# A hybrid attention trunk on one core: gate projections one pair ahead, zeros multiplied first, another place for one load

## The chip, the cores and the metric

One core of a Trainium2 chip runs the whole kernel. The metric is the time of one execution on the device, in microseconds (us); lower is better. Engines are named as in the profile: PE is TensorE (PEld its weight loads), DVE VectorE, ACT ScalarE, POOL GpSimd, SP the engine whose queue issues the DMAs.

## The reference

1024 tokens of width 1024 pass through two residual layers and a final RMSNorm. The first layer, in which the change lies, is

```python
h = rmsnorm(x, norm_w[0])
qa, ka, va, qb, kb, vb, z = jnp.split(h @ w_in, splits, axis=-1)
oa, _ = banded_attention(qa, ka, va, bias_a, band_a, sinks)          # 8 heads, window 128
for window, dil in ((128, 1), (512, 4), (2048, 16)):                 # 8 heads, dilated
    o, lse = banded_attention(to_strided(qb, dil), to_strided(kb, dil), to_strided(vb, dil), ...)
ob = sum(softmax(lses) * outs)
x = x + (concat([oa, ob]) * silu(z)) @ w_out
```

Each branch output is multiplied by a gate, silu of the projection z, before the output projection. The second layer is multi-head latent attention with 16 heads and a gate of its own.

## The kernel before, in words

**Precision.** Every large product is made of three matmuls: each operand is split into a high part and a rest, and `mm3` (lines 116 to 118) adds high x high, rest x high and high x rest in one bank of PSUM. A split is a copy on ACT (line 96) and a subtraction on DVE (101, 103) or POOL (111).

**First phase, to about 94 us.** For each of 8 blocks of 128 tokens: load x (`load_x`, line 322), sum of squares on ACT (124), a power on POOL (126), scaling on DVE (129), eight transposes on PE (137), the split into hH and hL, and the value projection of the dilated heads (24 matmuls into `ot`), which goes to DRAM. The eight weight tiles of that projection (`load_v`, 311) are loaded during block 0; the load of block 1 is issued after the sixth of them. DVE also makes the tables of sines and cosines in this phase.

**Projections.** `tproj` makes one 128-column projection of all tokens: two weight loads (`wst`), splits of them, and 8 blocks x 3 products x 2 halves of the tokens = 48 matmuls of 512 columns into `tp`. `proj_qk(pr)` makes q and k of a pair of heads (96 matmuls for the first four pairs, 48 for the last four), `proj_z(pr)` its gate (48, then tanh on ACT, line 178, and a product on DVE, 179).

**Heads.** There are 8 pairs. The dilated heads are pairs 0 to 3, the sliding-window heads pairs 4 to 7. A dilated head has eight groups of scores (four natural, four strided); a group is four matmuls into one bank `sc` (lines 225 and 226), per region of the bank a reduction on DVE that adds the bias and finds the maximum (229), and an exponential on ACT (232) that frees the bank; there are two such banks. Then the two softmaxes are merged: a small matmul (601), vector work, and a second small matmul (628), called the merge matmul here, whose result DVE reads as x (630). The values follow: POOL scales the probabilities (237), PE transposes them (188, bank `pt`), ACT and DVE split the transposes (96, 101), and PE multiplies by v (204, bank `ot`).

**Order.** Work is written as lists of pieces. At step n the values of head n are interleaved with the scores of head n+1, and the list `fill` is the projection work that PE can do meanwhile: q and k of the next pair at even n, the gate of the own pair at odd n, the gate of pair 7 at n = 14. The table `WAIT` holds some pieces of `fill` back behind named matmuls. A scheduler then places the pieces on the engines' queues by its own model of their durations; what order came out is shown below. Each engine takes its queue in order. `finish(pr)` multiplies the gate into the pair's output and stores it.

**Buffers.** The pool `gp` has one buffer for a gate, `sp` two for the natural bias `b1` and two for its copy `b1r`. A table of 128 x 824 numbers is loaded as `pm`, of which 4 and 32 columns are used.

Of the kernel before, what the change touches and what calls it, by code (L numbers as in the profile page):

```python
# [20 lines left out]
SEQ = 1024  # L21
P = 128
# [269 lines left out]
def layer0(c, x, norm_w, rel_bias, w_in, w_out, onehot, band, perm, x1d, tables, before_out, x1_done):  # L292
# [12 lines left out]
    with tc.tile_pool(name="ph1", bufs=1, reuse_waits="tile", side="right") as p1:  # L305
# [20 lines left out]
        for t in range(NT):  # L326
            xs = p1.tile([P, D], F32, name="xs", tag="xs", bufs=2)
            rms_rows(c, p1, xts[t], w0, xs, xs, 1 if t else 2)
            to_hT(c, xs, t, hH, hL)
            if t == 0:  # L330
                for d in range(ND):
                    load_v(d)
                    if d == 5:
                        load_x(1)
            elif t + 1 < NT:
                load_x(t + 1)
            ps = c.bank("ot")
            m = None
            tt = slice(t * P, (t + 1) * P)
            for d in range(ND):  # L340
                m = c.mm3(ps, hH[:, d, tt], hL[:, d, tt], wv[d][0], wv[d][1], d == 0, d == ND - 1, m)
            vt = p1.tile([P, 8, P], F32R, name="vt", tag="vt", bufs=2)
            src = ps.rearrange("p (h e) -> p h e", h=8)
            c.copy(vt[:, :, :HD], src, 0.5)
            c.low(vt[:, :, HD:], src, vt[:, :, :HD], 0.5)
            dma.dma_start(vd[tt], f(vt))
# [32 lines left out]
    def tl(pool, shape, dt, tag, bufs):  # L379
        return pool.tile(shape, dt, name=tag, tag=tag, bufs=bufs)  # L380

    pm = sp.tile([P, 4 * P + 312], F32, name="pm")
    dma.dma_start(pm, perm)


    o = 4 * P
    quarter, unsel = pm[:, o + 8:o + 12], pm[:, o + 24 + 192 + 64:o + 24 + 192 + 96]
    same = sp.tile([P, R4, RA], F32, name="same")
    V.tensor_reduce(same[:, 0], c.ident.rearrange("p (b a) -> p a b", a=RA), axis=AX.X, op=ALU.add)
    V.tensor_copy(same[:, 1:], same[:, 0:1].to_broadcast([P, R4 - 1, RA]))  # L390
    same = same.rearrange("p r a -> p (r a)")

    def bias_tile(h, cfg, tag, quarters=False):
        b = tl(sp, [P, 256], F32, tag, 2)
        o = wr.offset + (cfg * 16 + h) * P * 384 + 127
        if quarters:
            for r in range(R4):
                dma.dma_start(b[r * RA:(r + 1) * RA], bass.AP(wr.tensor, o + 383 * r, [[4 * 383, RA], [1, 256]]))
        else:
            dma.dma_start(b, bass.AP(wr.tensor, o, [[383, P], [1, 256]]))  # L400
        return b
# [92 lines left out]
    def proj_z(pr):  # L494
        e = pairs[pr]

        def alloc():
            e["gate"] = tl(gp, [P, SEQ], F32, "gate", 1)
        col = pr * P + (512 if pr < 4 else -512)
        return [alloc] + tproj(c, hH, hL, w_in, Z_COL + col, lambda hf, ps, s: gate_evac(c, e["gate"])(hf, ps, s))  # L500

# [24 lines left out]
    def head_a(pr, ei):  # L526
# [2 lines left out]
        e, pts, d = pairs[pr], [], {}  # L529

        def begin():
            d["bias"] = bias_tile(h, 0, "b1")
            st = tl(sp, [P, 32], F32, "sta", 2)
            d["neg"], d["den"], d["es"], d["rr"] = [st[:, 8 * i:8 * i + 8] for i in range(4)]
            d["parts"] = banded(c, pts, e["q"][ei], lambda a, b: [e[n][ei][:, a * P:b * P] for n in ("k", "kl")], d["bias"],
                                d["neg"], d["den"], c.negsink[:, h:h + 1])
            d["parts"][0]()
# [203 lines left out]
    for i in (3, 8):  # L741
        fill[i] = behind(c, fill[i], lambda: first)
    interleave(fill)
    interleave(heads[0][0])
    interleave(heads[0][2])
    wo = []

    WAIT = {1: {1: 6, 2: 6, 3: 6, 4: 6}, 3: {1: 3, 2: 3, 3: 3, 4: 3}, 5: {4: 0}, 8: {4: 7}, 12: {3: 0, 4: 2}}
    for n in range(16):
# [4 lines left out]
            pairs[7]["split"] = [op0.tile([P, SEQ], F32R, name=f"g7{i}") for i in "hl"]  # L754
            wsplit = [lambda d=d, hf=hf: split_wo(d, hf) for hf in range(2) for d in range(ND)]
        elif e:
            fill = proj_z(pr)
        else:
            fill = (kv_a() if pr == 3 else []) + (proj_qk(pr + 1) if pr < 7 else proj_z(7))
        if n == 13:  # L760
            fill += [lambda d=d: load_wo(d) for d in range(ND)]
        pv = heads[n][1]
# [550 lines left out]
def trunk(tc, x, positions, norm_w, rel_bias, ab_w_in, ab_sinks, ab_w_out, c_w_in, c_q_norm, c_w_qb, c_kv_norm,  # L1313
          c_w_kvb, c_w_out, final_norm, ident, onehot, band, perm, cmask, invf, out):
    c = Ctx(tc)
    with ExitStack() as es:
# [2 lines left out]
        c.cpool = es.enter_context(tc.tile_pool(name="const", bufs=1, reuse_waits="tile", side="left"))  # L1319
        c.ident = c.cpool.tile([P, P], F32, name="ident")  # L1320
        c.dma.dma_start(c.ident, ident)
        c.mhalf = c.cpool.tile([P, 1], F32, name="mhalf")
        c.V.memset(c.mhalf, -0.5)
        x1d = tc.dram_tile([SEQ, D], F32, name="x1d")
# [94 lines left out]
```

## Time and profile before

| what | value |
|---|---|
| median of 3 runs | 1135.27 us (1132.24 to 1136.85) |
| the profiled execution's own time | 1138.69 us |
| its span, first to last instruction | 1136.9 us |
| PE busy | 1083.2 us, 95% of the span |
| DVE, ACT, POOL busy | 662.3, 589.3, 499.2 us |
| share of the chain that ended last | PE 79%, DVE 6%, ACT 5%, DMA 5% |

PE's busy time counts overlapping matmuls as one stretch, and a matmul at the lower clock is busy for longer; so idle time and granted clock (PEclk, 1.00 is 2.4 GHz, 0.50 is 1.2 GHz) are read together, stretch by stretch. The heads of the first layer run from about 94 to 490 us, the second layer from about 580 us to the end.

### The profile page before, as it was taken

Reading aid. Unit: us, or ns where it says so; the run is one execution under the profiler, and the core shown is the slowest. Engines: PE = TensorE matmul, PEld = TensorE weight load, DVE = VectorE, ACT = ScalarE, POOL = GpSimd, SP = SyncE. Lnnn points to the kernel's source line nnn. Section 1 sums busy time; section 2 is a strip of 40 time slices with the busy share of each in tenths; the row PEclk is TensorE's granted clock in tenths of the full one; section 3 lists DMA queues with packets and bytes.
Section 4 is the critical chain, followed back from the end, with each engine's and each line's share of the span. In section 5 each row is a group of like instructions: output and inputs, shape, how many; then the busy total and the mean of one; then the engine's idle time right before and its main releaser. Section 6 shows DMA issues by size and latency. Waiting matters only on the chain.

```text
span 1136.9 us, 17458 instructions
## 1 busy us (share of the span) xinstructions
PE 1083.2 (95%) x5974; PEld 923.6 (81%) x5974; DVE 662.3 (58%) x1645; ACT 589.3 (52%) x1419; POOL 499.2 (44%) x543
## 2 busy tenths in 40 slices
PE   6998999999999999899999999899999999988997
PEld 4776878788888888678889988779887888777786
DVE  6534655565655656743332332688887898785323
ACT  5335555455645656732223322677777777685211
POOL 3112453455444454642123124365755665576301
PEclk9999899899999999899999999999999999999999
DMA  8848225142242321165222020132302311620311
GB/s 300 268 145 166 52 63 139 45 119 79 57 132 64 119 63 43 35 204 164 79 90 52 10 66 28 47 79 67 84 5 66 74 38 29 176 75 19 111 74 74
DMA packets 86359, 102.43 MB, mean 90 GB/s; under 512 B 7216, under 2 KB 70224, under 8 KB 86272
## 3 DMA queue, kind: packets, MB, share of 16 engines
q1 hardware_dynamic: 86272, 101.33, 31.8%
q8 instruction: 47, 0.77, 0.3%
q14 instruction: 40, 0.33, 0.1%
HBM read 67.97 MB, written 21.28 MB: 79 GB/s over the span
## 4 chain that ended last, share of the span: by engine, by line
PE 79%; DVE 6%; ACT 5%; DMA 5%; issue 3%; POOL 1%; SPq 0%; POOLq 0%; ACTq 0%; DVEq 0%
PE tp L116 14%; PE tp L118 14%; PE tp L117 14%; PE ot L204 8%; PE pt L188 7%; PE sc L1123 3%; PE sc L1124 2%; PE sc L1125 2%; PE sc L225 2%; PE ot L118 2%; PE ot L116 2%; PE ot L117 2%; PE sc L226 2%; PE pt L116 1%; PE pt L118 1%
## 5 line engine op out<-in xcount | busy, mean ns | idle before, releaser
L237 POOL TENSOR_TENSOR pc<-pc,ast 128x896 f32<-128x896 f32 (+7 forms) x128 | 145.5, 1154 | 114.2 <-DVE ast L1136 104.5
L116 PE MATMUL tp<-hH,wh 128*128 128x512 f32 x480 | 191.5, 399 | 1.3 <-DVE q L103 0.7
L118 PE MATMUL tp<-hH,wl 128*128 128x512 f32 x480 | 190.0, 396 | 0.0
L117 PE MATMUL tp<-hL,wh 128*128 128x512 f32 x480 | 189.9, 396 | 0.0
L101 DVE TENSOR_TENSOR ptl<-pt,pth 128x512 fp32r<-128x512 f32 (+2 forms) x248 | 157.5, 643 | 50.2 <-ACT pth L96 46.3
L96 ACT ACTIVATE pth<-pt 128x512 fp32r<-128x512 f32 (+2 forms) x248 | 135.7, 563 | 77.4 <-PE pt L188 71.1
L204 PE MATMUL ot<-pth,vt 128*128 128x128 f32 (+2 forms) x488 | 133.9, 307 | 7.3 <-ACT pth L96 6.0
L111 POOL TENSOR_TENSOR wl<-wst,wh 128x512 fp32r<-128x512 f32 x60 | 79.2, 1326 | 125.7 <-ACT wh L96 114.8
L204 PE MATMUL ot<-ptl,vt 128*64 128x128 f32 (+2 forms) x488 | 118.6, 288 | 4.9 <-DVE ptl L101 4.7
L1134 ACT ACTIVATE pc<-sc,ast 128x896 f32<-128x896 f32 (+7 forms) x128 | 94.9, 742 | 28.2 <-DVE ast L1132 22.4
L204 PEld LDWEIGHTS ot<-pth,vt 128*128 128x128 f32 x488 | 90.6, 196 | 19.9 <-ACT pth L96 10.0
L116 PEld LDWEIGHTS tp<-hH,wh 128*128 128x128 f32 x480 | 91.0, 190 | 19.0 <-PE tp L118 1.1
L118 PEld LDWEIGHTS tp<-hH,wl 128*128 128x128 f32 x480 | 90.8, 189 | 17.2
L1132 DVE CUSTOM_DVE_ANT_0 sc<-sc,mask 128x256 f32<-128x256 f32 (+7 forms) x128 | 97.2, 760 | 12.9 <-PE sc L1125 6.8
L117 PEld LDWEIGHTS tp<-hL,wh 128*128 128x128 f32 x480 | 91.0, 190 | 16.5
L188 PE MATMUL pt<-ident,pc 128*128 128x128 f32 x576 | 89.5, 276 | 1.1 <-POOL pc L237 0.9
L204 PEld LDWEIGHTS ot<-ptl,vt 128*128 128x128 f32 (+1 forms) x488 | 78.3, 170 | 15.1 <-DVE ptl L101 8.7
L237 POOL TENSOR_TENSOR p<-p,fac 128x256 f32<-128x256 f32 (+1 forms) x128 | 65.3, 549 | 49.3 <-DVE e L621 42.5
L1123 PE MATMUL sc<-kh,qh 96*128 96x384 f32 (+4 forms) x192 | 72.5, 378 | 4.9 <-ACT pc L1134 3.8
L188 PEld LDWEIGHTS pt<-ident,pc 128*128 128x128 f32 x576 | 68.2, 142 | 7.2 <-POOL pc L237 1.4
L96 ACT ACTIVATE wh<-wst 128x512 fp32r<-128x512 f32 x60 | 37.9, 632 | 64.6 <-PE tp L117 34.2
L1124 PE MATMUL sc<-kl,qh 96*128 96x384 f32 (+4 forms) x192 | 66.0, 345 | 1.7 <-DMA kl<-kd 1.7
(325 smaller groups left out, 2464.5 us busy)
## 6 DMA issues: line engine op xcount, KB each, us to landing
wst<-in_ab_w_in_dram SPq DMA_DIRECT2D x44, 256.0 KB, 3.4
kh<-kh SPq DMA_DIRECT2D x17, 256.0 KB, 3.4
kl<-kl SPq DMA_DIRECT2D x17, 256.0 KB, 4.1
xt<-in_x_dram SPq DMA_DIRECT2D x8, 512.0 KB, 6.5
vd<-vt SPq DMA_DIRECT2D x8, 512.0 KB, 3.7
vt<-vd SPq DMA_DIRECT2D x32, 128.0 KB, 3.4
vt<-vd SPq DMA_DIRECT2D x8, 512.0 KB, 5.2
xr<-in_x_dram SPq DMA_DIRECT2D x8, 512.0 KB, 4.3
```

Source lines behind the costliest of these rows:

```text
L96: return self.S.activation(out, in_, AF.Copy, scale=scale)
L101: return self.V.tensor_tensor(out, in_, f(high), op=ALU.subtract)
L116: m = self.order(after, self.order(prev, self.T.matmul(ps, lh, rh, start=start, stop=False)))
L117: m = self.order(m, self.T.matmul(ps, lh, rl, start=False, stop=False))
L118: return self.order(m, self.T.matmul(ps, ll, rh, start=False, stop=stop))
L188: c.T.transpose(ps[:, i * P:(i + 1) * P], s, c.ident)
L204: m = self.c.mark = self.c.T.matmul(out, lhsT, rhs, start=self.first is None, stop=stop, skip_group_check=True)
L237: c.scaled = c.G.tensor_tensor(ap, ap, factor.to_broadcast(list(ap.shape)), op=ALU.mult)
L1123: m = c.order(m, T.matmul(o, qh[0:96, q], kh[0:96, k0:k1], start=True, stop=False))
L1124: m = c.order(m, T.matmul(o, qh[0:96, q], kl[0:96, k0:k1], start=False, stop=False))
L1132: V.tensor_tensor_reduce(out=ps, in0=ps, in1=mask[:, SEQ - n:], scale=-1.0, scalar=BIG, op0=ALU.add, op1=ALU.min, accum_out=neg)
L1134: S.activation(pt, ps, AF.Exp, bias=neg, scale=-1.0, accum_out=den)
```

## The change

1. **Gates.** The eight gate projections are made as lists beforehand. That of pair 0 is placed right after the scores of the first head. At odd n the gate of the next pair is the fill for pairs 0 to 3. The gates of pairs 5, 6 and 7 (three lists of five pieces) are cut into four parts, for n = 9, 11, 13 and 14; each part holds 36 matmuls, where 48 stood at each of these steps. The gate has two buffers.
2. **Zeros.** Sixty matmuls of a 128 x 128 tile of bfloat16 zeros are put first on PE, into a bank that nothing reads.
3. **Load.** The load of block 1 is issued after the third value weight and not after the sixth.
4. **Room.** The table `pm` is replaced by two tiles of the columns that are used; the natural bias has one buffer, and the sliding-window heads use `b1r`.

```diff
-                    if d == 5:
+                    if d == 2:
                         load_x(1)
...
-    pm = sp.tile([P, 4 * P + 312], F32, name="pm")
-    dma.dma_start(pm, perm)
+    quarter, unsel = sp.tile([P, R4], F32, name="quarter"), sp.tile([P, 32], F32, name="unsel")
+    dma.dma_start(quarter, perm[:, 4 * P + 8:4 * P + 12])
+    dma.dma_start(unsel, perm[:, 4 * P + 280:4 * P + 312])
...
-        b = tl(sp, [P, 256], F32, tag, 2)
+        b = tl(sp, [P, 256], F32, tag, 1 if quarters else 2)
...
-            e["gate"] = tl(gp, [P, SEQ], F32, "gate", 1)
+            e["gate"] = tl(gp, [P, SEQ], F32, "gate", 2)
...
-            d["bias"] = bias_tile(h, 0, "b1")
+            d["bias"] = bias_tile(h, 0, "b1r")
...
+    gates = [proj_z(pr) for pr in range(8)]
     interleave(heads[0][0])
     interleave(heads[0][2])
+    interleave(gates[0])
+    late = gates[5] + gates[6] + gates[7]
...
-            fill = proj_z(pr)
+            fill = gates[pr + 1] if pr < 4 else late[4 * pr - 16:4 * pr - 12]
         else:
-            fill = (kv_a() if pr == 3 else []) + (proj_qk(pr + 1) if pr < 7 else proj_z(7))
+            fill = (kv_a() if pr == 3 else []) + (proj_qk(pr + 1) if pr < 7 else late[12:])
...
+        zeros = c.cpool.tile([P, P], BF16, name="zeros")
+        c.V.memset(zeros, 0.0)
+        c.warm = c.psum.tile([P, HALF], F32, name="tp", tag="tp")
+        for _ in range(60):
+            c.T.matmul(c.warm[:, :P], zeros, zeros, start=True, stop=True)
```

How the order moves is shown at three places. A row is line, operation, tile written, tiles read, shape. First ACT, at the first exponentials of the first head (`p<-sc`), before and then now:

```order
L232 ACT_TABLE_LOAD
L232 ACTIVATE p_808,nat<-sc,nat 128x128
L232 ACTIVATE p_808,nat<-sc,nat 128x256
L232 ACTIVATE p_818,nat<-sc,nat 128x256 x2
L96 ACTIVATE kh<-tp 64x4x128
L96 ACTIVATE wh<-wst 128x512
L232 ACTIVATE p_828,nat<-sc,nat 128x256 x2
L232 ACTIVATE p_838,nat<-sc,nat 128x256 x2
L96 ACTIVATE wh<-wst 128x512
L96 ACTIVATE kh<-tp 64x4x128
```

```order
L232 ACT_TABLE_LOAD
L232 ACTIVATE p_873,nat<-sc,nat 128x128
L232 ACTIVATE p_873,nat<-sc,nat 128x256
L232 ACTIVATE p_883,nat<-sc,nat 128x256 x2
L178 ACTIVATE gate<-tp 128x512
L96 ACTIVATE wh<-wst 128x512
L232 ACTIVATE p_893,nat<-sc,nat 128x256 x2
L232 ACTIVATE p_903,nat<-sc,nat 128x256 x2
L96 ACTIVATE wh<-wst 128x512
L178 ACTIVATE gate<-tp 128x512
```

The two halves of the first gate (L178) stand where the two halves of the next pair's k stood, and k follows later. On PE, between the first score matmul and the first merge matmul, 79 projection and 51 score matmuls stood; now 131 and 52 do. From there to the next run of ten projection matmuls there is no projection work to speak of, before or now, and eight more score matmuls now (60 for 52).

Second PE, around the merge matmul (L628) of the fourth head, before and then now (`ot` are values, `pt` transposes, `tp` projections):

```order
L225 MATMUL sc<-kh,qn 128x256
L226 MATMUL sc<-kl,qn 128x256
L225 MATMUL sc<-kh,qn 128x256
L226 MATMUL sc<-kl,qn 128x256
L628 MATMUL pt<-u,same 128x32
L204 MATMUL ot<-pth,vt 128x128 x2
L188 MATMUL pt<-ident,p_1670 128x128 x3
L188 MATMUL pt<-ident,p_1687 128x128
L204 MATMUL ot<-ptl,vt 64x128
```

```order
L118 MATMUL tp<-hH,wl 128x512
L628 MATMUL pt<-u,same 128x32
L116 MATMUL tp<-hH,wh 128x512
L117 MATMUL tp<-hL,wh 128x512
L118 MATMUL tp<-hH,wl 128x512
L116 MATMUL tp<-hH,wh 128x512
L117 MATMUL tp<-hL,wh 128x512
L118 MATMUL tp<-hH,wl 128x512
L116 MATMUL tp<-hH,wh 128x512
L204 MATMUL ot<-pth,vt 128x128 x2
L117 MATMUL tp<-hL,wh 128x512
```

The next head's eight score matmuls stood right ahead of the merge matmul and now stand behind the next eight transposes; ten projection matmuls precede the merge matmul, and eighteen stand between it and those transposes. Third SP, at the start, before and then now:

```order
L322 DMA xt<-in_x_dram 128x1024
L325 DMA nw<-in_norm_w_dram 128x1024
L311 DMA vst<-in_ab_w_in_dram 128x512 x6
L322 DMA xt<-in_x_dram 128x1024
L311 DMA vst<-in_ab_w_in_dram 128x512 x2
```

```order
L322 DMA xt<-in_x_dram 128x1024
L325 DMA nw<-in_norm_w_dram 128x1024
L311 DMA vst<-in_ab_w_in_dram 128x512 x3
L322 DMA xt<-in_x_dram 128x1024
L311 DMA vst<-in_ab_w_in_dram 128x512 x5
```

Three value weights move behind the second block's x.

## Rows read from the trace of the kernel before

**Rows 1.** Stretches: length, busy us of PE, PEld, DVE, ACT, POOL; PEclk, DMA, GB/s.

```profile
93.80:126.10 32.30, 28.00 (x134) 22.81 (x134) 17.42 (x68) 18.27 (x59) 11.10 (x15) 0.89 0.57 110
126.10:153.60 27.50, 23.84 (x162) 22.05 (x162) 20.38 (x82) 18.76 (x64) 16.77 (x31) 0.81 0.29 72
...
197.00:215.00 18.00, 15.45 (x80) 12.81 (x79) 11.27 (x31) 8.67 (x20) 12.99 (x22) 0.81 0.23 63
215.00:470.00 255.00, 254.44 (x1569) 223.35 (x1568) 146.94 (x457) 146.16 (x418) 119.69 (x170) 1.00 0.27 78
```

**Rows 2.** Waits of PE, 93.8 to 126.1 us: total, times, longest.

```profile
PE sc L225 <- ACT p L232: 3.5, 4, 2.0
```

**Rows 3.** Timeline of PE: start us, us, engine, line, operation, tiles, shapes.

```profile
101.24 0.39 PE L117 MATMUL tp<-hL,wh 128*128 128x512 f32 x1
101.47 0.28 PE L225 MATMUL sc<-kh,qn 128*128 128x256 f32 x1
101.59 0.29 PE L226 MATMUL sc<-kl,qn 128*128 128x256 f32 x1
```

**Rows 4.** Line 232, 93.8 to 126.1 us: duration ns min/median/max, first and last start.

```profile
L232 ACT ACTIVATE p<-sc,nat x14: 369/466/477, 99.0 to 121.3; 128x256 f32<-128x256 f32 x12, 128x128 f32<-128x128 f32 x2
```

**Rows 5.** The page: groups (busy, mean ns, idle before); issues (KB, us to landing).

```profile
L111 POOL TENSOR_TENSOR wl<-wst,wh 128x512 fp32r<-128x512 f32 x60 | 79.2, 1326 | 125.7 <-ACT wh L96 114.8
...
wst<-in_ab_w_in_dram SPq DMA_DIRECT2D x44, 256.0 KB, 3.4
```

**Rows 6.** Tile sc, 126.1 to 153.6 us: duration ns min/median/max.

```profile
L229 DVE CUSTOM_DVE_ANT_0 sc<-sc,b1r x10: 300/432/465, 125.7 to 145.4; 128x256 f32<-128x256 f32 x9, 128x128 f32<-128x128 f32 x1
```

**Rows 7.** Timeline of PE at the fourth head's merge matmul; idle before in brackets.

```profile
203.09 0.30 PE L628 MATMUL pt<-u,same 128*128 128x32 f32 x2
...
205.71 0.63 PE L188 MATMUL pt<-ident,p 128*128 128x128 f32 x4 [1.61 <-DVE x L630]
```

**Rows 8.** Timeline of DVE in the same microseconds.

```profile
202.82 0.30 DVE L229 CUSTOM_DVE_ANT_0 sc<-sc,b1r 128x128 f32<-128x128 f32 x1 [1.02 <-PE sc L226]
...
203.21 1.41 DVE L103 SCALAR_TENSOR_TENSOR q<-tp,q 64x512 fp32r<-64x512 f32 x2
204.64 0.43 DVE L229 CUSTOM_DVE_ANT_0 sc<-sc,b1r 128x256 f32<-128x256 f32 x1
...
204.99 0.47 DVE L229 CUSTOM_DVE_ANT_0 sc<-sc,b1r 128x256 f32<-128x256 f32 x1
...
205.38 0.19 DVE L630 TENSOR_TENSOR x<-pt,pm 128x32 f32<-128x32 f32 x1
```

**Rows 9.** Timeline of SP: start us, us for all of the issues.

```profile
2.11 3.26 SPq L311 DMA_DIRECT2D vst<-in_ab_w_in_dram  x6
```

**Rows 10.** The chain that ended last: start us, us, what.

```profile
5.42 7.28 DMA xt<-in_x_dram
...
14.87 2.30 DVE xs L129
...
37.69 0.50 PE ot L118
...
85.38 9.31 DMA wst<-in_ab_w_in_dram
```

**Rows 11.** Stretches, 10 to 38 us; columns as in rows 1.

```profile
10.00:38.00 28.00, 26.28 (x107) 18.47 (x107) 25.32 (x54) 16.28 (x31) 11.02 (x11) 1.00 0.84 283
```

**Rows 12.** Timeline of PE, short matmuls at 1.2 GHz, and projections of block 0.

```profile
15.07 0.63 PE L116 MATMUL ot<-wvh,hH 128*128 128x512 f32 x1
15.49 0.63 PE L117 MATMUL ot<-wvl,hH 128*128 128x512 f32 x1
...
138.24 0.57 PE L204 MATMUL ot<-pth,vt 128*128 128x64 f32 x2
138.63 0.40 PE L204 MATMUL ot<-ptl,vt 128*64 128x64 f32 x2
138.84 0.56 PE L225 MATMUL sc<-kh,qn 128*128 128x256 f32 x1
```

More of the change, by code (lines that the diff above doesn't have):

```diff
@@ L380, in tl @@
         return pool.tile(shape, dt, name=tag, tag=tag, bufs=bufs)
-    pm = sp.tile([P, 4 * P + 312], F32, name="pm")
-    dma.dma_start(pm, perm)
-    o = 4 * P
-    quarter, unsel = pm[:, o + 8:o + 12], pm[:, o + 24 + 192 + 64:o + 24 + 192 + 96]
+    quarter, unsel = sp.tile([P, R4], F32, name="quarter"), sp.tile([P, 32], F32, name="unsel")
+    dma.dma_start(quarter, perm[:, 4 * P + 8:4 * P + 12])
+    dma.dma_start(unsel, perm[:, 4 * P + 280:4 * P + 312])
     same = sp.tile([P, R4, RA], F32, name="same")
```

## The prediction

> **What bounds the kernel now.** The table of stretches comes first [rows 1]. For each stretch it gives TensorE's busy time and the clock it was granted. A stretch's loss is its idle time plus the share of clock withheld times its length: "0.89" over 32.3 us means that 3.55 us went in running at 1.2 GHz where 2.4 was to be had. From 215 to 470 us, where the later heads run, the loss is 0.56 us in 255: TensorE is the bound there, and a matmul taken out gives its time back. Three stretches around the first heads are different.
>
> - 93.8 to 126.1 us (first head's scores): 4.30 idle + 0.11 x 32.3 = 3.55, together **7.9 us**.
> - 126.1 to 153.6 us (first head's values beside the second head's scores): 3.66 + 0.19 x 27.5 = 5.2, together **8.9 us**.
> - 197 to 215 us (from the third head to the fourth): 2.55 + 0.19 x 18 = 3.4, together **6.0 us**.
>
> The clock falls only in stretches in which TensorE waits. The table of waits says for what: in the first of them, scores wait 3.5 us for the exponentials that free their bank [rows 2]. TensorE takes its instructions in order, so projections queued behind such a score wait too.
>
> The times of one instruction are starts in the timeline [rows 3]: from a projection matmul to the next instruction 0.23 us, from a score matmul to the next 0.12 us. The first stretch checks: its order holds 79 projection and 51 score matmuls, 79 x 0.23 + 51 x 0.12 = 24.3 us, and 32.3 - 7.9 = 24.4.
>
> **The change part by part.** The sum is made against the profiled execution, 1138.7 us (span 1136.9), which is 3.4 us above the median of the runs, 1135.3.
>
> *Gates one pair ahead.* One gate projection is 8 blocks x 3 products x 2 halves = 48 matmuls, 48 x 0.23 = 11.0 us. The order of the changed program has 131 projection and 52 score matmuls in the first stretch: the same work plus one gate. That is 131 x 0.23 + 52 x 0.12 = 36.4 us of work. With much more between two groups of scores, a bank's exponentials (two of 0.47 us [rows 4]) are long done when the next group comes; I leave 1.0 us of loss, so the stretch is 37.4 us, **+5.1**. The bounds are 36.4 (+4.1) and 36.4 plus the whole old loss (+12.0). The other engines have room: the gate adds to ScalarE two tanh and two splits, to POOL two of the 1.33 us subtractions [rows 5], and ScalarE was busy 18.3 of 32.3 us, POOL 11.1, VectorE 17.4 [rows 1].
>
> The other end: heads 9, 11, 13 and 14 now get 36 projection matmuls each and not 48, so 4 x 12 x 0.23 = **-11.0**, at full price, since that region has no loss. Thinner cover may open a hole there: I take **+2**, between 0 and 6.0, one hole as long as the loss at 197 to 215.
>
> *126.1 to 153.6.* No projection stands there before or after, and the values' work is the same. Eight score matmuls more do: four regions, each a 0.43 us reduction on VectorE [rows 6], 4 x 0.43 = +1.7. They leave the dense part behind it, -8 x 0.12 = -1.0. Together **+0.7**; bounds -3 (a third of the loss goes, say with the clock) and +4 (each region costs a full 0.9 us of reduction and exponential).
>
> *197 to 215.* In the old order the merge matmul at 203.09 stands behind eight score matmuls, and the transposes that follow it wait 1.61 us for VectorE's x [rows 7]. VectorE does that x only at 205.38, because two q evictions and three score reductions stand before it in its queue [rows 8]. In the new order, seven projection matmuls follow the merge, then values, then eleven more, and only then transposes: some 4 us of cover for a wait of 2.3. The scores come after. I take **-5.0** of the 6.0; bounds 0 and -6.0.
>
> *Second block's load.* Six weight loads are issued in 3.26 us ahead of it, 0.54 each [rows 9]; now three are, so it goes 1.6 us earlier. It is in the chain that ended last: the load to 12.7, the sum of squares, the scaling at 14.87, then VectorE almost without a break until TensorE takes over at 37.69 [rows 10]. VectorE was idle 28.0 - 25.3 = 2.7 us from 10 to 38 [rows 11], so no more than that can be gained. The three weight loads behind it come later by one transfer and hold up the first block's values. **-1.5**; bounds 0 and -2.7.
>
> *Zeros.* The sixty matmuls begin when VectorE has cleared the tile, at about 0.9 us. No such instruction is in the trace. Nearest are those with 128 or fewer columns while 1.2 GHz was granted: 0.105 and 0.195 us [rows 12]. I take the lower (128 columns at 1.2 GHz), so they end at 0.9 + 60 x 0.105 = 7.2 us, before the first transposes at 8.2: cost 0. By the upper they end at 12.6, and the first block is up to 4.3 late. In return the matmuls from 12 to 16 us, 0.42 apart now [rows 12], could run at 0.23: ten of them, 2.0 us. I count 0 of it, because TensorE is in the chain only from 37.69 [rows 10]. The Trainium skill says otherwise: its page "TensorE: Matmul & The Clock Gate" (section "Why this matters for your kernels") has TensorE kept busy beforehand so that it is past the slow state when real work comes; by that rule the 2.0 would be gained as well.
>
> *Edits with one answer.* The table of 128 x 824 numbers becomes two small loads; it lies behind the first blocks' loads, so 0. The natural bias has one buffer, so a bias load on SP's queue waits for the copy of the previous head's bias, with weight loads queued behind it. Heads are some 20 us apart, and a load lands in 2 to 4: 0.
>
> Sum: +5.1 - 11.0 + 2 + 0.7 - 5.0 - 1.5 + 0 = **-9.7**, so 1129.0 for the profiled execution and **1125.6** against the median.
>
> **The rivals.**
>
> - *The late heads do not give it back* (chance 0.15). If heads 9 to 14 are bound by their own chain of scores, exponentials and transposes, 48 matmuls less there shorten nothing: +5.1 + 0.7 - 5.0 - 1.5 = -0.7, 1134.6 us. Against it: 254.4 busy of 255 us at full clock, VectorE 147, ScalarE 146 [rows 1]. For it: the Trainium skill ("Trainium Kernel Development and Optimization", section "Performance Expectations") holds busy time of matmuls to be a poor measure, since they overlap, and points to the weight loads' share. That share is 223.4 of 255, high as well, so the trace is with my reading.
> - *Slower: thin cover opens holes* (0.07). Each of the four thinner slots could become what 197 to 215 was, a late vector result, idle time and then a lowered clock, 6.0 us each. Four cost 24.0 in place of my 2: 1125.6 + 22.0 = 1147.6. It decides from two on: 12.0 - 2 = 10.0 eats the gain.
> - *The cover does not come where the order puts it* (0.10). The first stretch now needs three projections' weights in a row. One weight load took 9.31 us from issue, behind the value loads [rows 10]. If the third pair is as late against the usual 3.4 [rows 5], TensorE waits 5.9, less the 1.0 allowed: -4.8, 1130.5.
> - *The start is TensorE's after all* (0.10). With the clock up from the first token on, the 2.0 us comes on top: 1123.6. The Trainium skill's rule above is this case. Against it: the engine stands idle again between the zeros' end and the tokens.
>
> **How the numbers follow.** My forecast has 0.58. A measurement of this kernel tells about 0.5% (5.7 us) from no change. Within the forecast some 0.51 lies beyond that on the fast side; with 0.10 of the clock rival and 0.05 of the two others, faster is 0.66. Slower is the thin cover's 0.07 and a tail of 0.01: 0.08; the rest, 0.26, is within. The range: the forecast with its bounds partly added reaches from 1117.5 (scores' stretch, hole and start all near their good ends, -8) to some 1131. Taking in late weights and the gain that is not given back, it ends at 1134.5.
>
> **What would show it.** Right: between the first score and the first merge matmul, TensorE without the 3.5 us of waits and at full clock, some 37 us long; no fall of the clock near the fourth head's merge; the scaling of the second block near 13.3 and not 14.87; from the fourth pair on the same instructions some 5 us later at first and 9 earlier at the end of the heads. The second stretch should still show its loss. Wrong: new waits on exponentials or transposes between heads 9 and 14, a lowered clock there, a wait on weights in the first stretch, or zeros that still run when the first transposes are ready.

## The result, and the profile after

The changed kernel took 1142.75 us, median of 4 runs (1140.79 to 1144.43), the kernel before 1135.34 beside it: ratio 1.0068, interval 1.0042 to 1.0095. Timed again among the experiments it was 1.0049 (1.0031 to 1.0067). It is slower by 6 to 7 us where 9.7 faster was forecast, beyond the range's end of 1134.5.

Both kernels were profiled twice. The two pairs of executions differ by 2.1 us (1140.79, the lowest of its kernel, against 1138.69, 3.4 above the median of its own) and by 7.7 us (1144.75 against 1137.02). The table has the starts of TensorE's landmarks; "parts" is the difference from one landmark to the next.

| landmark | before | after | before, again | after, again | parts, both pairs | forecast |
|---|---|---|---|---|---|---|
| first score | 93.86 | 95.33 | 92.79 | 96.34 | +1.5, +3.6 | -1.5 |
| first merge matmul | 126.09 | 132.97 | 125.92 | 134.83 | +5.4, +5.4 | +5.1 |
| second | 146.90 | 157.49 | 146.91 | 159.33 | +3.7, +3.5 | +0.7 |
| eighth | 332.98 | 341.60 | 333.36 | 343.49 | -2.0, -2.3 | -5.0 |
| last transposes ahead of the second layer | 586.08 | 585.95 | 586.60 | 587.80 | -8.7, -8.9 | -9.0 |
| end | 1136.92 | 1139.01 | 1135.22 | 1142.97 | +2.2, +6.6 | 0 |

The heads repeat within 0.3 us from pair to pair; start and second layer do not. A stretch's loss is counted as the prediction counts it, idle time plus the share of the clock that was withheld. The stretches of the changed kernel that answer to [rows 1] (columns as there):

```profile
95.33:132.97 37.64, 36.87 (x186) 30.82 (x185) 19.17 (x69) 21.75 (x65) 12.33 (x13) 1.00 0.53 112
132.97:157.49 24.52, 18.98 (x110) 16.19 (x108) 18.95 (x68) 13.66 (x52) 13.79 (x26) 0.73 0.21 57
203.00:213.00 10.00, 10.00 (x55) 8.39 (x54) 5.60 (x15) 3.50 (x6) 8.05 (x16) 1.00 0.61 140
213.00:225.00 12.00, 9.58 (x56) 8.12 (x55) 4.89 (x14) 5.32 (x14) 4.86 (x7) 0.86 0.31 79
```

**First head's scores: as forecast.** 0.77 us idle and full clock, where 7.9 were lost (1.65 idle in the second profile). The waits of [rows 2] are gone; in 95.3 to 133 the changed kernel's waits of TensorE are this row:

```profile
PE tp L116 <- DVE q L103: 0.8, 1, 0.8
```

**Second stretch: worse.** 5.54 idle and 0.27 x 24.52 = 6.6 withheld by the clock are 12.2 us; from 126.09 to 146.90 the kernel before lost 20.81 - 18.09 = 2.7 and, at a clock of 0.75, 5.2:

```profile
126.09:146.90 20.81, 18.09 (x113) 16.83 (x113) 15.45 (x63) 13.46 (x44) 10.08 (x18) 0.75 0.27 70
```

One wait makes most of the new idle time. Here it is in the timelines of TensorE, VectorE and GpSimd:

```profile
144.26 0.47 PE L204 MATMUL ot<-ptl,vt 128*64 128x128 f32 x2 [2.97 <-DVE ptl L101]
```

```profile
140.41 3.33 DVE L592 TENSOR_TENSOR u<-own,quarter 128x16 f32<-128x16 f32 x1
143.66 0.54 DVE L101 TENSOR_TENSOR ptl<-pt,pth 128x384 fp32r<-128x384 f32 x1
...
144.33 0.25 DVE L592 TENSOR_TENSOR u<-own,quarter 128x16 f32<-128x16 f32 x2
```

```profile
139.94 3.76 POOL L237 TENSOR_TENSOR p<-p,fac 128x128 f32<-128x128 f32 x8
```

A VectorE product of 16 columns, two of which take 0.25 us a little later, took 3.33 us: it ends (143.74) when GpSimd's eight scalings end (143.70). The split that the values wait for stands right behind it. In the kernel before the same scalings had run from 129.25 to 133.0 and met no such product; its longest there was 0.82 us for two:

```profile
134.64 0.82 DVE L592 TENSOR_TENSOR u<-own,pm 128x16 f32<-128x16 f32 x2
```

The Trainium skill, page "GPSIMD Engine Reference" (section "Architecture"), says that GpSimd's physical SBUF read and write port are both shared with VectorE; the trace agrees with that here, and shows a price of 3.2 us for one small instruction (one such product alone takes 0.17 us at 144.85).

The price is not paid each time. Nine more executions of the list below have the gates ahead, the same product in the same place and 3.3 us for it, each time ending 0.03 to 0.04 us behind the scalings. In e11 and e15 TensorE has e4's order, and the product again starts 0.5 us into the eight scalings; it took 0.53 and 0.51 us. VectorE and GpSimd in e15, and the stretch between the two merge matmuls in e4 (product 3.32 us) and in e15:

```profile
138.49 0.51 DVE L593 TENSOR_TENSOR u<-own,quarter 128x16 f32<-128x16 f32 x1
137.99 3.76 POOL L237 TENSOR_TENSOR p<-p,fac 128x128 f32<-128x128 f32 x8
```

```profile
128.74:153.25 24.51, 18.99 (x109) 16.19 (x108) 18.95 (x68) 13.65 (x52) 13.78 (x26) 0.72 0.22 58
131.03:151.89 20.86, 18.06 (x110) 15.11 (x109) 16.53 (x68) 13.72 (x52) 13.78 (x26) 0.78 0.24 67
```

So the held product is what the second stretch lost: 23.2 to 24.5 us in the ten executions with it, 20.9 in e15 and 20.4 in e11, about what the kernel before took (20.8). What decides whether it is held is open; the overlap alone does not. Nor is the first stretch the same in every kernel with the gates ahead: it lasted 36.6 to 38.5 us in ten executions, but 40.3 in e11 and 40.5 in e13.

**Fourth head: the loss moved.** From 203 to 213 us nothing is lost; from 213 to 225 it is 2.42 idle and 0.14 x 12 = 1.7. VectorE and TensorE there:

```profile
215.43 1.41 DVE L103 SCALAR_TENSOR_TENSOR q<-tp,q 64x512 fp32r<-64x512 f32 x2
216.87 0.43 DVE L229 CUSTOM_DVE_ANT_0 sc<-sc,b1r 128x256 f32<-128x256 f32 x1
...
217.22 0.46 DVE L229 CUSTOM_DVE_ANT_0 sc<-sc,b1r 128x256 f32<-128x256 f32 x1
...
217.60 1.28 DVE L101 TENSOR_TENSOR ptl<-pt,pth 128x512 fp32r<-128x512 f32 x2
```

```profile
218.34 0.33 PE L204 MATMUL ot<-ptl,vt 128*64 128x128 f32 x2 [1.91 <-DVE ptl L101]
```

That is [rows 8] with another victim: the q evictions and reductions that x stood behind now stand ahead of the split ptl, and TensorE waits 1.91 us for it in place of 1.61 for x.

**Start.** The zeros end at 6.0, and block 1 is scaled at 13.04 in place of 14.87, as forecast:

```profile
0.99 5.01 PE L1331 MATMUL tp<-zeros 128*128 128x128 bf16 x60 [0.99 <-DVE zeros L1328]
```

```profile
13.04 2.28 DVE L129 SCALAR_TENSOR_TENSOR xs<-xt,rstat,nw 128x1024 f32<-128x1024 f32 x1 [0.73 <-POOL rstat L126]
```

But TensorE, done earlier with block 1, then waits 1.71 us for block 2, and the last block's norm (line 126) comes at 61.33 where it came at 59.88. GpSimd in the changed kernel:

```profile
60.73 0.63 POOL L563 COPY b1r<-b 128x256 f32<-128x256 f32 x1 [12.31 <-DMA b<-wr]
61.33 0.55 POOL L126 TENSOR_TENSOR rstat<-rstat,mhalf 128x1 f32<-128x1 f32 x1
```

### The profile page after: what moved, and what is told of

It reads as the page before. It is cut to its first block, busy times and chain, and to the rows that moved or that the text cites. A ratio compares the mean times of both kernels' runs of the same rounds, so it can differ in the third digit from the quotient of the medians.

```text
span 1139.0 us, 17588 instructions
## 1 busy us (share of the span) xinstructions
PE 1085.3 (95%) x6034; PEld 924.7 (81%) x6034; DVE 665.1 (58%) x1646; ACT 589.1 (52%) x1419; POOL 501.0 (44%) x543
## 4 chain that ended last, share of the span: by engine, by line
PE 79%; DVE 7%; ACT 4%; DMA 4%; issue 3%; POOL 1%; SPq 0%; POOLq 0%; ACTq 0%; DVEq 0%
PE tp L116 14%; PE tp L118 14%; PE tp L117 14%; PE ot L204 8%; PE pt L188 7%; PE sc L1127 3%; PE sc L1128 2%; PE sc L1129 2%; PE sc L225 2%; PE ot L118 2%; PE sc L226 2%; PE ot L116 2%; PE ot L117 2%; DMA vd<-vt 2%; PE pt L116 1%
## 5 line engine op out<-in xcount | busy, mean ns | idle before, releaser
L1129 PE MATMUL sc<-kh,ql 96*128 96x384 f32 (+4 forms) x192 | 67.0, 349 | 0.2 <-DVE ql L103 0.2
```

Of the source, the lines that this page charges most:

```text
L1129: m = c.mark = c.order(m, T.matmul(o, ql[0:96, q], kh[0:96, k0:k1], start=False, stop=True))
```

## The experiments

Three theories stood at first: A, the start costs; B, the gates ahead cost; C, the zeros bring the clock up earlier and it is paid back nowhere. All results in one table; the last three columns are us of each kernel's one profiled execution: the first score, the time from there to the last transposes ahead of the second layer ("heads"), and the second layer.

| run | ratio to before, interval | first score | heads | second layer |
|---|---|---|---|---|
| kernel before; again (e16) | | 93.86; 92.79 | 492.2; 493.8 | 550.8; 548.6 |
| changed kernel | 1.0068, 1.0042 to 1.0095 | 95.33 | 490.6 | 553.1 |
| e1 zeros | 1.0017, 1.0008 to 1.0026 | 93.75 | 491.7 | 552.7 |
| e2 load | 1.0014, 1.0001 to 1.0027 | 93.12 | 489.6 | 552.2 |
| e3 room | 1.0010, 0.9993 to 1.0027 | 94.06 | 492.7 | 553.0 |
| e4 gates, room | 0.9998, 0.9984 to 1.0011 | 92.15 | 489.4 | 552.7 |
| e5 changed kernel again | 1.0049, 1.0031 to 1.0067 | 96.34 | 491.5 | 555.2 |
| e6 gates, room, load | 1.0061, 1.0045 to 1.0077 | 97.16 | 488.9 | 552.9 |
| e7 gates, room, zeros | 1.0028, 1.0018 to 1.0037 | 93.29 | 489.4 | 555.6 |
| e8 zeros, load | 0.9998, 0.9982 to 1.0015 | 93.58 | 491.9 | 551.0 |
| e9 room, load | 1.0045, 1.0027 to 1.0062 | 98.59 | 491.8 | 552.0 |
| e10 changed, copies behind | 1.0014, 0.9998 to 1.0030 | 96.12 | 488.0 | 553.1 |
| e13 changed, four vt | 1.0060, 1.0041 to 1.0079 | 96.58 | 494.7 | 553.2 |
| e14 changed, both | 1.0038, 1.0024 to 1.0052 | 95.22 | 489.4 | 554.8 |
| e11 as e4, copies behind | 0.9985, 0.9973 to 0.9998 | 92.17 | 488.9 | 552.2 |
| e15 as e4, both | 0.9996, 0.9982 to 1.0011 | 93.22 | 487.7 | 552.4 |
| e12 as e11, pieces held | 0.9985, 0.9969 to 1.0001 | 92.06 | 490.5 | 552.5 |
| e18 as e11, late slots full | 0.9988, 0.9977 to 0.9999 | 92.12 | 488.8 | 550.6 |
| e17 as e7, two turns | 1.0010, 0.9997 to 1.0024 | 92.60 | 490.7 | 553.2 |

### One part at a time (e1 to e4)

Each is the kernel before with one or two numbered items of the change: e1 item 2, e2 item 3, e3 item 4, e4 items 1 and 4. The whole edit of e2, for one:

```diff
-                    if d == 5:
+                    if d == 2:
```

> Only the sixty zero matmuls are added to the kernel before. Theory A (the start costs: the value phase of the changed kernel ended 1.5 us later): about 0.5 to 1.5 us slower, ratio 1.0005 to 1.0015, the first score at about 95.3 in place of 93.9 if the zeros are what delays it. Theory B (the gates ahead cost): ratio 1.000, within 0.1%. Theory C (the clock comes up earlier and is paid back nowhere): first block's projections 0.23 apart in place of 0.42, first score within 0.5 us of 93.9, ratio 0.998 to 1.000.

> Only the place of the second block's load is changed. Forecast of the prediction: 1.5 us faster (0 to 2.7). Theory A: the scaling of block 1 comes 1.8 us earlier, but the value weights behind it come later and TensorE waits for their splits instead, so the first projection of block 1 is where it was or later; first score at 93.9 to 95.3, ratio 1.000 to 1.0015. Theory B: ratio 1.000, as the whole loss is in the heads.

> Only the buffers are changed (two small loads for the table, one natural bias buffer, the sliding-window heads on the other bias tag). The prediction has 0 for it. Theory A and B: ratio 1.000 within 0.1%. A rival (the bias load waits in SP's queue with weight loads behind it): 1 to 4 us slower, with waits on weight splits in the heads.

> Gates one pair ahead with the room they need, without zeros and with the old place of the load. Theory A (the start costs): first score at 93.9, and the whole is 1.5 to 3 us faster than the changed kernel, ratio to the kernel before 1.003 to 1.005. Theory B (gates ahead cost everything): ratio 1.006 to 1.008, the merge matmul of head 1 some 10 us after that of the kernel before, and nothing given back in heads 9 to 14. Prediction's own sum for this part: -8.2 us, ratio 0.993.

The gates with their room cost nothing and gain nothing: B falls, and so does the forecast's -8.2 for them. A is not seen in a single part either: the first scores are at 92.2 to 94.1, and the kernel before has 92.8 and 93.9. Of C the clock's part came (in e1 block 0's projections are 0.23 us apart, [rows 12] has 0.42), and no gain with it. No part alone costs over 2 us, and they sum to +0.0029 (0.0017 + 0.0014 - 0.0002), about half of what the whole costs. So the parts act on each other.

### Two parts at a time (e5 to e9)

Edits: the items named in the table, nothing else.

> The changed kernel once more, beside its own parts on one chip. If parts add (zeros +2.0, load +0.8, gates with room -0.2 us in the runs so far): 1.002 to 1.003. If they act on each other: 1.006 to 1.007 as measured first.

> Gates with their room, and the load in its new place; no zeros. Theory A2 (the earlier load moves the copies of the bias rows behind each other: the store of the values lands some 17 us after its issue, behind 3 MB of bias rows, and the value phase ends 1.5 to 3 us later than with the gates alone): first score at 93.6 to 95.3 where the gates alone have 92.2, ratio 1.002 to 1.004. Rival Z (the zeros do it): ratio 1.000, first score at 91.5 to 92.2.

> Gates with their room, and the zeros; the load in its old place. Theory A2: first score at 92.2, ratio 1.000 to 1.002. Rival Z: ratio 1.004 to 1.007.

> Zeros and the new place of the load, gates in the old place. If the two work together against each other at the start: first score at 94.5 or later and ratio 1.004 or more. If each only adds its own: ratio 1.002 to 1.003. If the extra loss needs the gates (a thinner cover behind the later start): 1.001 to 1.002.

> Room and the new place of the load alone; gates in the old place, no zeros. Theory Q: with one natural bias buffer the copy of the first bias (line 563) stands ahead of the last block's norm (line 126) in POOL's queue and waits for the 3 MB of bias rows; the earlier load makes those rows go out some 3 to 4 us later, so the norm is at 61 to 63 us in place of 58 to 60, the first score 34.0 us behind it at 95 to 97, and the ratio is 1.003 to 1.007, without any gate. Rival (the gates are needed for the loss): first score at 94 or earlier, ratio 1.000 to 1.003.

The load costs where the room is (e9 and e6 against e3 and e4: first score 4.5 and 5.0 us later) and not where it isn't (e2, e8). No gate is needed. The zeros cost nothing with the load alone (e8, 0.9998, is below all that was expected of it) and 3 us on the gates (e7, between the two theories); on gates and load together they cost nothing that shows (e6 has 1.0061 without them, the changed kernel 1.0068 and 1.0049). Of theory A2 the direction held, its size was too small for e6.

The loss begins at the wait for block 2. TensorE in e9, then two stretches of e9 and the same two of e3 (columns as in [rows 1]):

```profile
28.07 0.39 PE L117 MATMUL ot<-wvl,hH 128*128 128x512 f32 x1
30.15 0.80 PE L118 MATMUL ot<-wvh,hL 128*128 128x512 f32 x1 [1.68 <-DVE hL L101]
...
31.17 0.63 PE L117 MATMUL ot<-wvl,hH 128*128 128x512 f32 x1
31.59 0.63 PE L118 MATMUL ot<-wvh,hL 128*128 128x512 f32 x1
```

```profile
28.00:32.00 4.00, 2.32 (x6) 1.52 (x6) 4.00 (x14) 0.81 (x3) 0.05 (x1) 0.66 0.77 246
32.00:36.00 4.00, 4.00 (x12) 3.10 (x11) 2.96 (x6) 0.00 (x0) 1.82 (x2) 0.50 0.37 104
```

```profile
28.00:32.00 4.00, 4.00 (x19) 2.65 (x18) 3.58 (x13) 1.85 (x4) 0.64 (x1) 1.00 0.83 269
32.00:36.00 4.00, 4.00 (x23) 3.30 (x21) 3.84 (x13) 2.57 (x6) 2.50 (x3) 1.00 0.55 187
```

With the old place of the load, block 1's projections last to 27.9 and VectorE has split block 2's first half at 28.8, before the first product that reads the split (x19 and x23 matmuls, never idle). With the new place they are done by 25.5 and the split only at 30.1; TensorE does what it can of block 2 and then stands idle, and behind that the granted clock is 0.50 and projections are 0.42 to 0.43 apart. VectorE is busy 4.00 of 4.00 us in the idle stretch. In the changed kernel's first profile TensorE waits as long (1.71 us) at a clock of 1.00, and its first score is the earliest of the four executions with room and load so far. In all seven of them in the table the wait is 1.68 to 1.71 us; behind it the clock fell in six (1.7 us withheld in five, 3.4 in e9) and not in that one: the clock's part comes and goes, the wait does not. The wait by itself is not the loss: without room it is 1.19 us in e2 and 1.59 in e8, and with the old load and the zeros 1.69 in e7, each at 1.00, and their first scores are at 93.1 to 93.6.

How the loss gets from there to the first score, and why it needs the room, can be followed. The last of three bias matmuls (L360) is queued on TensorE behind block 2; in e9 VectorE waits 2.05 us for it, and the bias rows go out behind what it makes of it, at 40.98 in place of 38.18 in the changed kernel's first profile. GpSimd's copy of the first bias waits for these rows, and the last block's norm stands behind that copy: 64.63 in place of 61.33. The first score follows the norm by 34.0 us in the changed kernel (both profiles), e6, e9 and e13. In the kernel before, the norm stands behind such copies too, but the bias rows go out at 34.95. In e2 and e8, with the load and without the room, the order that came out has the norm ahead of the copies. VectorE and GpSimd in e9, then GpSimd in e2:

```profile
37.15 0.55 DVE L361 TENSOR_TENSOR ub<-sc,bm 16x384 f32<-16x384 f32 x1 [2.05 <-PE sc L360]
64.63 0.55 POOL L126 TENSOR_TENSOR rstat<-rstat,mhalf 128x1 f32<-128x1 f32 x1
```

```profile
55.95 0.55 POOL L126 TENSOR_TENSOR rstat<-rstat,mhalf 128x1 f32<-128x1 f32 x1 [7.94 <-DVE rstat L125]
61.56 0.64 POOL L563 COPY b1r<-b 128x256 f32<-128x256 f32 x1 [5.06 <-DMA b<-wr]
```

### What waits behind the bias rows (e10, e11, e13 to e15)

The replication of the bias (`wr`, in two transfers of 3 and 1.5 MB) goes out at 38 to 41 us in the kernels with room and load, at 35 to 37 with the old place of the load. Two things end with it: the copy of the first bias on GpSimd, ahead of the last norm, and the store of block 2's values, without which block 4's values (`vt`, two buffers) can't be evicted; ScalarE's next sum of squares stands behind that. e10, e11: the copies behind the norm. e13: four buffers. e14, e15: both.

```diff
-    c.G.tensor_tensor(st[:, 2:3], st[:, 1:2], c.mhalf, op=ALU.pow)
+    c.norm = c.G.tensor_tensor(st[:, 2:3], st[:, 1:2], c.mhalf, op=ALU.pow)
...
-            G.tensor_copy(b1.rearrange(...), nat.rearrange(...))
+            g = G.tensor_copy(b1.rearrange(...), nat.rearrange(...))
+            c.order(c.norm, g)
...
-            vt = p1.tile([P, 8, P], F32R, name="vt", tag="vt", bufs=2)
+            vt = p1.tile([P, 8, P], F32R, name="vt", tag="vt", bufs=4)
```

> The changed kernel with one order added: the bias copies on POOL behind the last block's norm. Theory Q: the norm at 56 to 57 us in place of 61.3, the first score at 92 to 93.5 in place of 95.3 to 96.3, 2 to 4 us faster than the changed kernel, ratio to the kernel before 1.002 to 1.004. Rival (the store of the values that lands 17 us late, or the weights, hold the last blocks anyway): first score at 95 or later, ratio 1.005 or more.

> Gates with room, the old load, no zeros, and the same added order. Theory Q: norm at 56 to 57 in place of 58.0, first score at 91 to 92.2, 0 to 1 us faster than the gates alone, ratio 0.998 to 1.000.

> The changed kernel with four buffers for the values' eviction (vt) in place of two, nothing else. If the two waits are in parallel (both end with the bias rows), taking one away alone changes little: the bias copy still stands ahead of the last norm, norm at 61 to 62, first score at 95 to 96, ratio 1.004 to 1.006. If the values' buffer alone holds the blocks: first score at 92 to 93, ratio 1.001 to 1.003.

> The changed kernel with both waits taken away: copies behind the last norm, and four vt buffers. Both in parallel: norm of the last block at 55 to 57, first score at 91.5 to 93.5, 3 to 5 us faster than the changed kernel, ratio 1.000 to 1.002. If something else ends with the bias rows (x of the last block, a weight): first score at 95 or later.

> Gates with room, old load, no zeros, and both waits taken away. Norm of the last block at 55 to 56.5 in place of 58.0; first score at 91 to 92, ratio 0.997 to 0.9985. If TensorE itself sets the pace of the last blocks: first score unchanged at 92.2, ratio as with the copies alone, 0.9985.

The two waits are parallel: with one gone the norm stays where it was, held by the other. GpSimd, then ScalarE in e10, and GpSimd in e14:

```profile
61.76 0.55 POOL L126 TENSOR_TENSOR rstat<-rstat,mhalf 128x1 f32<-128x1 f32 x1 [12.09 <-DVE rstat L125]
62.26 0.63 POOL L563 COPY b1r<-b 128x256 f32<-128x256 f32 x1
```

```profile
59.31 0.60 ACT L96 ACTIVATE vt<-ot 128x512 fp32r<-128x512 f32 x1 [8.40 <-DMA vd<-vt]
59.80 0.59 ACT L96 ACTIVATE hH<-pt 128x512 fp32r<-128x512 f32 x1
60.28 1.06 ACT L124 ACTIVATE xs<-xt 128x1024 f32<-128x1024 f32 x1
```

```profile
58.02 0.55 POOL L126 TENSOR_TENSOR rstat<-rstat,mhalf 128x1 f32<-128x1 f32 x1 [7.94 <-DVE rstat L125]
61.85 0.63 POOL L563 COPY b1r<-b 128x256 f32<-128x256 f32 x1 [3.27 <-DMA b<-wr]
```

With both gone the norm is 3.3 to 4.3 us earlier than in the changed kernel's two profiles, but the first score only 0.1 to 1.1: by then TensorE's own delay from block 2 is left (e14 against e15, 2.0 us later still; from 36 us to the first score TensorE is idle for no more than 0.3). So of theory Q the order of events is shown and most of its price is not. The time of e14 is 0.003 below the changed kernel's first ratio and 0.001 below its second.

Two times do not fit. e10 (1.0014) is clear of the changed kernel's two intervals on the fast side, though its norm (61.76) and its first score (96.12) are no earlier; and e14, which has its order and the buffers besides, is at 1.0038. Where e10's gain lies stays open. e15, with both waits gone from the old load, has its norm at 56.06 as expected and gained nothing (first score 93.22, ratio 0.9996).

### Cover, zeros and the second profile (e12, e16 to e18)

e12 holds pieces of the second pair's projections back, e17 puts the zeros in two banks, e18 gives the last two slots their 48 matmuls again:

```diff
-    WAIT = {1: {1: 6, 2: 6, 3: 6, 4: 6}, ...
+    WAIT = {0: {6: 2, 7: 4, 8: 6, 9: 9}, 1: {1: 6, 2: 6, 3: 6, 4: 6}, ...
...
-        c.warm = c.psum.tile([P, HALF], F32, name="tp", tag="tp")
-        for _ in range(60):
-            c.T.matmul(c.warm[:, :P], zeros, zeros, start=True, stop=True)
+        for _ in range(2):
+            c.warm = c.psum.tile([P, HALF], F32, name="tp", tag="tp")
+            for _ in range(30):
+                c.T.matmul(c.warm[:, :P], zeros, zeros, start=True, stop=True)
...
-            fill = gates[pr + 1] if pr < 4 else late[4 * pr - 16:4 * pr - 12]
+            fill = gates[pr + 1] if pr < 4 else {4: late[:3], 5: late[3:5], 6: gates[6]}[pr]
...
-            fill = (kv_a() if pr == 3 else []) + (proj_qk(pr + 1) if pr < 7 else late[12:])
+            fill = (kv_a() if pr == 3 else []) + (proj_qk(pr + 1) if pr < 7 else gates[7])
```

> As the kernel before it in this list, with the last four pieces (48 matmuls) of the second pair's projections held behind score pieces of the second head, so that 24 projection matmuls stand between the first and the second merge matmul where none stood, and 107 in place of 131 ahead of the first. Theory H (the second stretch loses 13 to 15 us because nothing covers its waits for split transposes, and its clock falls): loss from 130 to 160 us down by 4 to 6, loss in the first head's scores up by 0 to 2, ratio 0.995 to 0.998. Rival (the values' own chain of scaling, transposes and splits sets the length, covered or not): the stretch grows by the 5.5 us of the 24 matmuls, no gain, 0.998 to 1.001.

> The kernel before, a second profiled execution. If the first one (1138.7, above the median by 2.4) was unlucky in its clock: 1134 to 1137, with one of its lowered-clock stretches (108, 132, 207 or 474 us) shorter or missing, so that the gates' gain in the heads against it is 4 us or less and not 6. If not: within 1 us of the first at every merge matmul.

> Gates, room, old load, and the sixty zeros in two banks (thirty each), so that they take two turns of the two tp banks in place of one. Theory T (one turn shifts which of the two banks each later tp tile gets, and in the second layer a projection then lands on the bank that is still being read): the 1.4 us wait for gt near 710 us is gone, 133.0 us from the last xs transposes to the second layer's first scores in place of 134.1, and the ratio is 1.000 to 1.0015 in place of 1.0028. Rival (the zeros shift the time, not the bank): wait still there, ratio 1.002 to 1.004.

> Gates, room, old load, no zeros, bias copies behind the last norm; heads 13 and 14 have 48 projection matmuls again, 9 and 11 have 24 each. Prediction's term for the thin slots (+2): the loss from 410 to 500 us goes from 18.3 back to 15.7 or below, heads 9 and 11 stay without a hole, ratio 0.996 to 0.998 in place of 0.9985. Rival (the holes only move to heads 9 and 11): loss from 230 to 410 us up by 2 to 6 in place of it, ratio 0.9985 or more.

**e12.** Two stretches of e11, then of e12 (columns as in [rows 1]):

```profile
90.00:130.00 40.00, 38.09 (x182) 31.51 (x181) 17.52 (x62) 20.84 (x61) 10.62 (x11) 0.96 0.58 115
130.00:160.00 30.00, 25.89 (x179) 22.34 (x178) 24.58 (x100) 21.39 (x74) 21.26 (x39) 0.89 0.27 71
```

```profile
90.00:130.00 40.00, 35.70 (x173) 29.37 (x171) 19.63 (x75) 21.78 (x67) 11.19 (x13) 0.96 0.55 112
130.00:160.00 30.00, 28.05 (x172) 25.03 (x173) 20.77 (x63) 15.05 (x43) 19.89 (x36) 0.83 0.24 62
```

The idle time goes with the cover: 1.91 and 4.11 us in e11, 4.30 and 1.95 in e12, the sum as before and the clock no better. At the eighth merge matmul e12 is 1.8 us behind e11 (338.63 for 336.86). No gain over e11 (0.9985 both): the rival's ratio.

**e16.** The first profile was not unlucky. The second execution of the kernel before took 1137.02 us and has the same falls of the clock in the heads; the merge matmuls are within 0.4 us of the first's. The gates' missing gain is not an accident of one profile.

**e17.** The zeros' bank does matter, though nothing reads it. In the second layer, where TensorE's order in e7 is that of e4, a projection waited for the reading of its bank; the changed kernel has the same row at 715.08. TensorE in e7, then in e17:

```profile
711.88 0.38 PE L116 MATMUL tp<-wvh,cH 128*128 128x256 f32 x1 [1.41 <-DVE gt L179]
```

```profile
712.43 0.50 PE L116 MATMUL pt<-cH,wkh 128*128 128x512 f32 x1 [0.70 <-DVE gt L179]
```

One turn more, and the 1.41 us wait is gone; one half as long takes its place on another bank (e1 has it too). The ratio falls from 1.0028 to 1.0010, though the intervals overlap. So which of two banks a tile gets, 700 us earlier, decides a wait.

All the profiles bear this out: the 1.41 us wait stands in all six executions that have the gates ahead and one turn of zeros (the changed kernel twice, e7, e10, e13, e14), and in none of the eleven without zeros; e1 and e8, zeros without the gates, have the 0.70. Behind the 1.41 the clock falls as well. The kernel before, then the changed kernel:

```profile
714.00:736.00 22.00, 18.75 (x105) 15.56 (x104) 17.70 (x38) 15.35 (x33) 7.16 (x7) 1.00 0.25 60
```

```profile
714.00:736.00 22.00, 18.79 (x90) 16.32 (x91) 15.10 (x33) 12.97 (x28) 6.68 (x7) 0.84 0.20 48
```

That is 0.16 x 22 = 3.5 us withheld; the second pair has the same two clocks there, 1.00 and 0.84.

**e18.** Neither side: the idle time from 410 to 500 us goes back, but so does the lowered clock. Stretch 410 to 500 us of e11, then of e18; the time is that of e11.

```profile
410.00:500.00 90.00, 81.17 (x449) 68.22 (x448) 60.42 (x123) 51.10 (x127) 48.34 (x51) 0.96 0.28 89
```

```profile
410.00:500.00 90.00, 83.67 (x452) 70.28 (x451) 59.88 (x124) 53.13 (x130) 46.29 (x51) 0.92 0.30 89
```

A version that clearly beats the kernel before was not found: e11 and e18 are 0.12% to 0.15% faster, less than the bound of 0.5%.

## Why the prediction was wrong

The steps that held: the first head's scores (+5.4 for +5.1, and for the reason given), the late slots (-8.7 and -8.9 for -9.0, in part by luck, as shown below), the zeros' end (6.0, the cheap bound 7.2), the scaling of block 1 (13.04 for 13.3). Of the rivals none came: no wait for weights stands in the first stretch, the late heads gave their matmuls back, the thin slots cost what was allowed.

The luck is in "at full price, since that region has no loss": the stretch of [rows 1] ends at 470 us, and the slots reach further. From 410 to 500 us, in the kernel before and then in the changed kernel:

```profile
410.00:500.00 90.00, 83.60 (x454) 70.18 (x453) 56.53 (x117) 53.03 (x130) 45.55 (x50) 0.92 0.23 73
```

```profile
410.00:500.00 90.00, 81.18 (x458) 68.28 (x457) 60.86 (x129) 55.14 (x136) 50.13 (x55) 0.96 0.26 82
```

The hole came as allowed: 8.8 us idle in place of 6.4, +2.4 for +2. But the clock rose from 0.92 to 0.96, 3.6 us less withheld, and no term has that. (Idle time at the lowered clock counts in both, so these parts do not simply add up to -8.7.)

Four things made the forecast wrong. The start (points 1 and 2) and the second layer (5) went beyond the bounds that they were given; the second stretch (3) and the fourth head (4) missed by some 3 us each within theirs. The steps that failed:

1. **"so no more than that can be gained ... -1.5"** (the load). The sum looked at how much earlier block 1 could be, and took the chain's VectorE part as if it ended earlier too. VectorE was no faster; TensorE's work was only done sooner, and the idle time came out between blocks 1 and 2. Measured: the load alone +0.0014 by ratio, its first score (93.12) between the two of the kernel before; 4.5 to 5.0 us lost there once the room edits are in.
2. **"Edits with one answer ... 0"** (the room). Priced by the bias load of the heads. What mattered was the queues at 35 to 65 us: the copy of the first bias, the 3 MB of bias rows that it waits for, the store behind them. With the load alone the last norm goes ahead of that copy, with load and room behind it. None of these had a row in the sum. Alone it is 1.0010 and not told from zero; with the load it is what the load's loss needs.
3. **"The values' work is the same ... +0.7"** (126 to 153 us). 3.7 and 3.5. The work was the same, but its meeting with another engine was not: the product u fell into GpSimd's scalings and took 3.33 us. Where it was not held (e11, e15) the stretch is within 0.6 us of the kernel before's.
4. **"some 4 us of cover for a wait of 2.3 ... -5.0"** (197 to 215 us). From the second merge matmul to the eighth 2.0 to 2.3 were gained. The wait for x went as said; what is late next behind the same VectorE instructions was not asked, and it is the split ptl.
5. **"cost 0"** (the zeros). Their time on TensorE is hidden, as said. Their turn of the banks is not: 1.41 us of wait in the second layer and 3.5 us withheld by the clock behind it. e7's second layer is 2.9 us longer than e4's, most of the 0.003 that e7 has over e4. The rival that TensorE's clock helps the start did not come: with zeros alone the first score (93.75) lies between the two of the kernel before, although block 0's projections did run 0.23 us apart.

Against the sum of -9.7 the two pairs of profiles miss by 11.8 and 17.5 us: the start 3.0 and 5.1, the second stretch 3.0 and 2.8, the fourth head 3.0 and 2.7, the late slots 0.3 and 0.1, the second layer 2.2 and 6.6. By the medians it is 16 to 17 us. Of the second layer's part, the wait of point 5 and the clock behind it are up to 4.9 us; the rest lies in falls of the clock that differ from execution to execution (from 1000 to 1045 us 0.92 and 1.00 in the two executions of the kernel before, 0.96 and 0.92 in those of the changed kernel), and what makes these differ **stays open**. In the kernels with gates and zeros the second layer took 553.1 to 555.6, with gates alone 550.6 to 552.9, without gates 548.6 to 553.0. Open too is how the start's loss divides: taking the two waits behind the bias rows away moved the first score by 1.1 us (e14 against the changed kernel's second profile, both with the clock lowered behind block 2), and the wait for block 2 with its lowered clock was not tried by itself. Nor was the fourth head's: that it is the split ptl is read from the timelines alone.

## What to carry to other kernels

Work moved ahead pays where TensorE truly had nothing to do; but a hole can have more candidates behind it in the slow engine's queue, and when the first is covered the next one in that queue can be late, here after the same evictions and reductions. Two edits that each cost nothing can share a transfer: look at what ends with the largest DMA of the phase, on every engine's queue, before calling an edit free. A dummy tile takes its turn of a buffer rotation, and later tiles get other banks.

## What was not expected of the hardware

A VectorE product of 16 columns with both inputs in SBUF took 3.33 us while GpSimd ran eight scalings, and ended with them within 0.04 us; two such products took 0.25 us when GpSimd had done. The same product at the same place took 0.53 and 0.51 us in e11 and e15, inside the same scalings. And the same stretch of code was granted a clock of 0.50 in e9 and 1.00 in the changed kernel's first execution, behind waits of the same length (1.68 and 1.71 us).
